# Moving both halves of a query product ahead of the last head's norm, and splitting the last output tile into column halves

## The chip, the cores and the metric

The kernel runs on one core of a Trainium2 chip. The core has five engines with instruction streams of their own: TensorE (PE in the profile; its weight loads are shown as PEld), VectorE (DVE), ScalarE (ACT), GpSimd (POOL) and SyncE (SP), which here only issues DMAs. The engines wait for each other by semaphores. The metric is the device time of one execution in microseconds (us); lower is better.

## The reference, cut to what matters

The kernel computes one layer of an encoder on 1024 tokens and 16 meta tokens, 1024 wide, in float32. Two branches, a neighbourhood attention with 8 heads and a gated recurrence (HGRN2) with 4 heads in both directions, share one input projection. Then come an output projection, an MLP and a last RMSNorm.

```python
def layer(h):                                   # h: (1040, 1024)
    a = rms_norm(h, norm_mix)
    q_na, k_na, v_na, q, z_f, z_b, i, g, gate_na, gate_hg = split(a @ w_in)
    y_na = neighbourhood_attention(q_na, k_na, v_na) @ w_na_out
    o = scan(q, z_f, i) + reverse(scan(reverse(q), ...))
    o = o * rsqrt(mean(o * o) + EPS)            # per head, 128 wide
    y_hg = (o * hg_norm * silu(g)) @ w_hg_out
    h = h + (sigmoid(gate_na) * y_na + sigmoid(gate_hg) * y_hg) @ w_o
    h = h + square(relu(rms_norm(h, norm_mlp) @ w_up)) @ w_down
    return rms_norm(h, norm_final)[16:]
```

## The kernel before, in words

**Products.** A float32 operand is split into a rounded part `hi` and a remainder `lo` (ACT makes `hi`, DVE makes `lo`), and each product is three matmuls, `hi*hi`, `hi*lo` and `lo*hi`, added up in one bank of PSUM (`mm3`, L120 to L124; `mm_pair`, L1395 to L1399). The widest matmul has 512 columns, which fill one bank. `aT[h]` is the normed input, transposed, for token half `h`.

**The join.** The kernel first computes the four recurrent heads (`hgrn`, a generator), then attention for four pairs of heads. At the join three things meet. The last head's tail normalizes its output: squares on ACT (L480), sums on DVE (L482), the root on POOL (L92, L93), the scaled `on` on DVE (L489), for two token halves; then PE transposes each half in four matmuls (`opt`, L493), DVE multiplies by gain and gate into `ot` (L495), and SP stores it (L498). `first_query` (L711) makes attention's first query product, one bank of 24 matmuls for each token half. Behind it come the key product of the first pair, in pieces of 256, 272 and 512 columns, the value product, and the scores (L825, read by DVE at L831).

Here the order on PE, ACT and DVE is the order in which the code is written (`manual_schedule`); on SP and POOL, and later in attention, a scheduler sets it. In every engine's queue an instruction that waits holds back all behind it. The banks of the projection rotate: `mm_cycle` lists two banks called `mm` and, in this stage, one called `mx`; each new product takes the next. A bank can be written again when its readers are done: for a query bank these are ACT's copies (`QX`, L766) and DVE's subtractions (L769). SP's queue holds the two stores of `ot`, then attention's bias (`bs`, L757) and mask (`NB`, L758); POOL subtracts the one from the other (L761), and forms block sums for a later stage (`rt`, L187 to L192).

**The end.** The MLP's second product runs in passes (`ps_` 0 to 3) over pieces of the hidden layer. The last pass adds up four row tiles of 128 rows, columns 512 to 1023, in four banks `bk[0][j]` (two `mm`, two `pa`). Its last two steps are held together (`tail` and `cur`), so that each row tile gets its last twelve matmuls in one go and can be finished while the next is multiplied. `acc[j, 0]` and `acc[j, 1]` hold the residual of the two column halves; `acc[j, 0]` is final long before, and POOL has already multiplied it by the norm's gain `g3` (`half_scaled`). What is left for each row tile is on several engines: DVE adds the bank (L1615), ACT squares and sums (`square`, L1511, a row for the square and one that reads the sum out), POOL adds the other half's sum (L1535) and takes the power -0.5 (L1536), ACT scales the first half (L1538), DVE the second (L1539), and SP stores both (L1540, L1541). On SP, DVE, ACT and POOL the order is again that of the code.

Of the kernel before, what the change touches and what calls it, by code (L numbers as in the profile page):

```python
# [9 lines left out]
F32 = mybir.dt.float32  # L10
F32R = mybir.dt.float32r
I32 = mybir.dt.int32
AF = mybir.ActivationFunctionType
ALU = mybir.AluOpType
# [4 lines left out]
P = 128  # L19
D = 1024  # L20
KC = D // P
T = 1024
TH = 512
# [25 lines left out]
def layer(ctx: ExitStack, tc: tile.TileContext, x, meta, w_in, w_na, w_hg, w_o, w_up, w_dn,  # L49
          g_mix, g_mlp, g_fin, gain, bias, lbl, lmask, wmask, out):  # L50
    nc = tc.nc
    pe, act, dve, pool, sp = nc.tensor, nc.scalar, nc.vector, nc.gpsimd, nc.sync
# [10 lines left out]
    mm_cycle = []  # L63
# [17 lines left out]
    half_c = cp.tile([P, 8], F32, name="half")  # L81
# [629 lines left out]
    def first_query():  # L711

        hi, lo = block_of(C_QN)
        early[C_KN] = block_of(C_KN)
        for h in range(2):
            ps = bank("mm", "mm").rearrange("p a b -> p (a b)")
            for k in range(KC):
                mm3(ps, hi[:, k], lo[:, k], *(t[:, k, :TH] for t in aT[h]), k == 0, k == KC - 1)
            yield ps
    in_order = ExitStack()  # L720
    in_order.enter_context(tc.manual_schedule(engines={e.engine for e in (pe, act, dve)}))
    query = first_query()
    query_ps = [next(query)]
    list(prev)
    query_ps += list(query)
    hps.close()


    gfs = ExitStack()
    gfp = gfs.enter_context(tc.tile_pool(name="gfp", bufs=1, side="right", reuse_waits="tile"))  # L730
    psum_pools(mx=1, s=2, t=2, b=1)
    mm_cycle[1:] = mm_cycle[:0:-1]

    with (tc.tile_pool(name="npr", bufs=1, side="right", reuse_waits="tile") as npr,
          tc.tile_pool(name="np", bufs=1, reuse_waits="tile") as npl):
# [17 lines left out]
        for p in range(NPAIR):  # L753
            NB = npl.tile([P, 2, 1024], F32, tag="NB", name="NB")
            for i in range(2):
# [3 lines left out]
                for o, j0, m in ((0, 0, 3), (432, 1, 2), (720, 0, 2)):  # L759
                    a = NB[:, i, o:o + m * SW].rearrange("p (j c) -> p j c", c=SW)[:, :, :P]  # L760
# [148 lines left out]
    def up_bank(t):  # L909
        return bank(t, t).rearrange("p a b -> p (a b)")  # L910
# [485 lines left out]
    def mm_pair(ps, a, b, q, j, first, last):  # L1396
        for n in range(3):
            pe.matmul(ps, a[n == 2][:, q, j * P:(j + 1) * P], b[n == 1][:, q],  # L1398
                      start=first and n == 0, stop=last and n == 2, skip_group_check=True)  # L1399
# [17 lines left out]
    def half(tag, dt=F32, bufs=1, name=None):  # L1417
        return fp.tile([P, TH], dt, tag=tag, name=name or tag, bufs=bufs)

    def two(tag, dt=F32, bufs=1):  # L1420
        return fp.tile([P, 2, TH], dt, tag=tag, name=tag, bufs=bufs)
# [103 lines left out]
    def half_scaled(i):  # L1525

        y = acc[i, 0]
        pool.tensor_tensor(y, y, g3[:, :TH], op=ALU.mult)
        acc[i, "part"] = fp.tile([P, 1], F32, tag="part", name="part", bufs=4)
        pool.tensor_scalar(acc[i, "part"], acc[i, "ssq"][:, 0:1], 1.0, EPS, op0=ALU.mult, op1=ALU.add)  # L1530

    def finish_half_scaled(i):
        rs = fp.tile([P, 1], F32, tag="rs", name="rs", bufs=4)
        tm = fp.tile([P, 1], F32, tag="rtm", name="rtm", bufs=4)
        pool.tensor_tensor(tm, acc[i, "ssq"][:, 1:2], acc[i, "part"], op=ALU.add)  # L1535
        pool.tensor_tensor(rs, tm, half_c[:, :1], op=ALU.pow)  # L1536
        y = [acc[i, hc] for hc in range(2)]
        act.mul(y[0], y[0], rs)  # L1538
        dve.scalar_tensor_tensor(y[1], y[1], rs, g3[:, TH:], op0=ALU.mult, op1=ALU.mult)  # L1539
        sp.dma_start(out[i * P:(i + 1) * P, :TH], y[0])  # L1540
        sp.dma_start(out[i * P:(i + 1) * P, TH:], y[1])  # L1541

    def after(ps_, bk):
        for j in range(4):
# [37 lines left out]
    with tc.manual_schedule(engines={sp.engine, dve.engine, act.engine, pool.engine}):  # L1582
        us = {n: fetch(*steps[n]) for n in (2, 3)}
        ready = prepare(*steps[2], us.pop(2))
        sp.dma_start(g3, g_fin.rearrange("(o d) -> o d", o=1).broadcast_to([P, D]))
        tail = None
        bk = bk0
        for n, (p_, m) in enumerate(steps):
            if n < 2:
                continue  # L1590
            cur = ready
            if n + 2 < len(steps):
                us[n + 2] = fetch(*steps[n + 2])
            if n + 1 < len(steps):
                ready = prepare(*steps[n + 1], us.pop(n + 1))
            if m == 0:
                bk = down_banks(2 if p_ < 3 else 1)
            if p_ < 3:
                multiply(p_, m, bk, cur)
                if m == NP - 1:  # L1600
                    after(p_, bk)
            elif m < NP // 2 - 2:
                a, b = cur
                for q in range(2):
                    for j in range(4):
                        mm_pair(bk[0][j], a, b, q, j, m == 0 and q == 0, False)
            elif tail is None:
                tail = cur
            else:

                for j in range(4):
                    for e, (a, b) in enumerate((tail, cur)):
                        for q in range(2):
                            mm_pair(bk[0][j], a, b, q, j, False, e == 1 and q == 1)
                    dve.tensor_tensor(acc[j, 1], acc[j, 1], bk[0][j], op=ALU.add)  # L1615
                    square(j, 1)
                    if j:
                        finish_half_scaled(j - 1)
                finish_half_scaled(3)
            side(p_, m)  # L1620


# [53 lines left out]
```

## Time and profile before

| what | value |
|---|---|
| median of three runs | 1527.96 us (1527.82 to 1528.82) |
| the profiled execution | 1527.06 us |
| its span, first to last instruction | 1525.3 us |
| mean granted TensorE clock | 0.999 of full speed |
| PE idle before `opt` (L493), over all four heads | 2.2 us, all ended by DVE's `on` (L489) |
| from 334.0 to 344.2 us: PE, DVE, POOL busy | 8.04, 4.76, 5.51 us |
| from 1518.3 to 1525.3 us: PE, DVE, ACT, POOL busy | 0, 2.10, 2.06, 0.74 us |

A row of the timeline gives the start (us from the span's start), the duration, the engine, the line and operation, what it writes from what it reads, and in brackets how long the engine stood idle before it and what ended that. A row of the groups gives the busy time and the mean duration in ns. The end of a matmul is modelled, and matmuls overlap, so the distance between two starts is the better measure of their cost. In a timeline row several neighbours of one kind can be merged (x4).

### The profile page before, as it was taken

The page shows a single profiled execution, that of the slowest core. Times are in us where ns is not written, and L with a number is a line of the kernel's source. Part 1 is how long each engine was busy: PE and PEld are TensorE (multiplying, and loading weights), DVE is VectorE, ACT ScalarE, POOL GpSimd, SP SyncE. Part 2 cuts the span into 40 slices and gives each one's busy share as a digit, 9 for nine tenths or more (in the row PEclk, how much of TensorE's full clock was granted, in tenths as well). Part 3 has the DMA queues.
Part 4 walks back from the last instruction along what each step waited for, and adds up shares of the span by engine and source line. Part 5 has one row for each costly group of instructions (what it writes and reads, how often), then busy time and mean ns, then how long its engine had stood idle before and what let it go on. Part 6 is the DMA issues. An engine that isn't in the chain of part 4 may idle for free.

```text
span 1525.3 us, 23529 instructions
## 1 busy us (share of the span) xinstructions
PE 1501.0 (98%) x9236; PEld 1254.6 (82%) x9236; DVE 1035.1 (68%) x1608; ACT 657.7 (43%) x1168; POOL 378.5 (25%) x355
## 2 busy tenths in 40 slices
PE   9999999999999999999999999999999999999998
PEld 8888888878888877888888887888888888888886
DVE  7876566655786777666485368877777544877876
ACT  6131313126665576334133235555555533434444
POOL 3313131324404400101000123433333200231142
PEclk9999999999999999999999999999999999999999
DMA  4211011113222227435656123544444676573224
GB/s 168 59 29 57 28 49 37 43 48 112 73 76 94 96 75 237 144 118 187 234 169 217 55 84 131 174 154 152 150 151 157 213 252 234 193 235 111 97 83 152
DMA packets 142591, 195.61 MB, mean 128 GB/s; under 512 B 8192, under 2 KB 90240, under 8 KB 142480
## 3 DMA queue, kind: packets, MB, share of 16 engines
q1 hardware_dynamic: 133216, 172.53, 34.5%
q10 hardware_dynamic: 7088, 14.24, 2.4%
q0 software_dynamic: 2176, 7.34, 1.3%
q8 instruction: 72, 1.18, 0.3%
q14 instruction: 39, 0.32, 0.1%
HBM read 139.56 MB, written 54.53 MB: 127 GB/s over the span
## 4 chain that ended last, share of the span: by engine, by line
PE 86%; DVE 5%; issue 3%; POOL 3%; ACT 2%; DMA 1%; SPq 0%; POOLq 0%; ACTq 0%; DVEq 0%
PE mm L122 10%; PE mm L123 10%; PE mm L124 9%; PE mm L1398 5%; PE pa L1398 4%; PE pb L905 4%; PE pb L906 4%; PE pb L907 4%; PE pb L1398 4%; PE pc L1398 4%; PE pc L905 3%; PE pc L907 3%; PE pc L906 3%; PE pa L905 2%; PE pa L906 2%
## 5 line engine op out<-in xcount | busy, mean ns | idle before, releaser
L122 PE MATMUL mm<-aT,hi 128*128 128x512 f32 (+2 forms) x600 | 214.5, 358 | 0.0
L124 PE MATMUL mm<-aT,lo 128*128 128x512 f32 (+2 forms) x600 | 212.3, 354 | 0.0
L123 PE MATMUL mm<-aT,hi 128*128 128x512 f32 (+2 forms) x600 | 211.3, 352 | 0.0
L97 DVE TENSOR_TENSOR dl<-ur,dh 128x1024 fp32r<-128x1024 f32 x54 | 71.0, 1315 | 87.4 <-ACT dh L96 85.6
L96 ACT CAST dh<-ur 128x1024 fp32r<-128x1024 f32 x54 | 56.9, 1054 | 166.5 <-issue 91.1
L122 PEld LDWEIGHTS mm<-aT,hi 128*128 128x128 f32 x600 | 113.2, 189 | 13.0
L124 PEld LDWEIGHTS mm<-aT,lo 128*128 128x128 f32 x600 | 113.2, 189 | 12.4
L123 PEld LDWEIGHTS mm<-aT,hi 128*128 128x128 f32 x600 | 113.3, 189 | 11.7
L112 ACT CAST hi<-raw 128x1024 fp32r<-128x1024 f32 x34 | 35.7, 1051 | 88.3 <-PE mm L123 78.1
L1203 DVE TENSOR_TENSOR wl<-raw,wh 128x512 fp32r<-128x512 f32 x50 | 40.9, 820 | 36.5 <-ACT wh L1202 36.4
L1207 ACT ACTIVATE uv<-uv 128x512 f32<-128x512 f32 x48 | 30.4, 633 | 80.0 <-DVE uv L1315 48.9
L1203 DVE TENSOR_TENSOR wl<-sx,wh 128x512 fp32r<-128x512 f32 x70 | 61.0, 881 | 3.4 <-ACT wh L1202 3.3
L1202 ACT CAST wh<-sx 128x512 fp32r<-128x512 f32 x70 | 42.2, 620 | 42.2 <-PE pc L906 24.0
L1488 POOL TENSOR_TENSOR w<-w,tt 128x512 f32<-128x512 f32 x16 | 23.4, 1461 | 132.9 <-DVE tt L1487 113.2
L300 POOL TENSOR_TENSOR Y<-X,TN 128x512 f32<-128x512 f32 x20 | 34.3, 1713 | 85.3 <-DVE X L297 85.3
L831 DVE CUSTOM_DVE_ANT_0 pr<-nsc,NB 128x432 f32<-128x432 f32 (+1 forms) x64 | 35.1, 558 | 29.1 <-issue 28.8
L409 DVE TENSOR_TENSOR QQ<-QQ,TN 128x512 f32<-128x512 f32 x48 | 35.1, 740 | 23.7 <-PE sc L404 23.7
L113 DVE TENSOR_TENSOR lo<-raw,hi 128x1024 fp32r<-128x1024 f32 x34 | 47.5, 1398 | 5.2 <-ACT hi L112 5.0
L905 PE MATMUL pb<-nt,wh 128*128 128x512 f32 x128 | 50.2, 392 | 0.3 <-DVE uv L1285 0.2
L122 PE MATMUL mm<-wh,mT 128*128 128x512 f32 x128 | 50.2, 392 | 0.0
L906 PE MATMUL pb<-nt,wh 128*128 128x512 f32 x128 | 49.9, 390 | 0.0
L907 PE MATMUL pb<-nt,wl 128*128 128x512 f32 x128 | 49.8, 389 | 0.0
(408 smaller groups left out, 4443.2 us busy)
## 6 DMA issues: line engine op xcount, KB each, us to landing
raw<-in_w_in SPq DMA_DIRECT2D x56, 512.0 KB, 3.9
ur<-usp SPq DMA_DIRECT2D x54, 512.0 KB, 3.6
raw<-in_w_up SPq DMA_DIRECT2D x16, 1024.0 KB, 6.0
usp<-us SPq DMA_DIRECT2D x60, 256.0 KB, 2.3
sg<-gsp SPq DMA_DIRECT2D x16, 512.0 KB, 4.0
w<-in_w_dn SPq DMA_DIRECT2D x16, 512.0 KB, 4.8
usp<-uv SPq DMA_DIRECT2D x30, 256.0 KB, 2.8
gsp<-gv ACTq DMA_DIRECT2D x24, 256.0 KB, 2.5
```

The lines of the kernel that those rows point to most:

```text
L96: act.copy(hi, src)
L97: dve.tensor_tensor(lo, src, hi.bitcast(F32), op=ALU.subtract)
L113: dve.tensor_tensor(lo[:, :kc], raw[:, :kc], hi[:, :kc].bitcast(F32), op=ALU.subtract)
L122: pe.matmul(ps, lh, rh, start=first, stop=False)
L123: pe.matmul(ps, lh, rl, start=False, stop=False)
L124: pe.matmul(ps, ll, rh, start=False, stop=last)
L905: pe.matmul(ps, lhs[0][:, c], rhs[0][:, k], start=first and k == 0, stop=False, skip_group_check=True)
L906: pe.matmul(ps, lhs[0][:, c], rhs[1][:, k], start=False, stop=False, skip_group_check=True)
L907: pe.matmul(ps, lhs[1][:, c], rhs[0][:, k], start=False, stop=k == 3, skip_group_check=True)
L1202: act.copy(v(hi), src)
L1203: dve.tensor_tensor(v(lo), src, v(hi).bitcast(F32), op=ALU.subtract)
L1398: pe.matmul(ps, a[n == 2][:, q, j * P:(j + 1) * P], b[n == 1][:, q], start=first and n == 0, stop=last and n == 2, skip_group_check=True)
```

## The change

There are two edits. At the join, both halves of `first_query` are now taken before the last head's tail is run (`list(prev)`); before, the second half stood behind it. The rotation of banks is changed with it: before `mm, mx, mm`, now `mx, mm, mm`.

At the end, the last row tile (row 3) is treated apart. Columns 768 to 1023 (`hi`) of its bank are added to `acc[3, 1]` before the last two steps are multiplied, and these steps' products for them go to a new bank of `pc`; columns 512 to 767 stay in the old bank. So the last tile's twelve matmuls of 512 columns become two groups of twelve of 256. The first group's part is added, squared and multiplied by the gain while the second group runs. The first part's sum of squares and that of the first column half go into one extra column of the second part's square: POOL forms their sum times 1024, its root is written as column 257, and ACT's square, which scales by 1/32, then sums all of it. One power follows, and the row is scaled in two pieces: 384 columns on ACT, 640 on DVE (`ylast`, in a tile tagged `tt`), each with one store, the first issued by ACT itself. In all rows the finishing of row j - 1 is now called ahead of the add and the square of row j (`between`).

```diff
-    query = first_query()
-    query_ps = [next(query)]
+    query_ps = list(first_query())
     list(prev)
-    query_ps += list(query)
     hps.close()
...
     psum_pools(mx=1, s=2, t=2, b=1)
-    mm_cycle[1:] = mm_cycle[:0:-1]
+    mm_cycle.insert(0, mm_cycle.pop())
...
-        pool.tensor_tensor(y, y, g3[:, :TH], op=ALU.mult)
+        if i < 3:
+            pool.tensor_tensor(y, y, g3[:, :TH], op=ALU.mult)
+        else:
+            pool.memset(root_c, 0.5)
+            ylast = ends["y"] = two("tt", bufs=2).rearrange("p q t -> p (q t)")[:, :D - SL]
+            pool.tensor_tensor(y[:, :SL], y[:, :SL], g3[:, :SL], op=ALU.mult)
+            pool.tensor_tensor(ylast[:, :P], y[:, SL:], g3[:, SL:TH], op=ALU.mult)
...
-    def finish_half_scaled(i):
+    def finish_half_scaled(i, between=lambda: None):
...
         act.mul(y[0], y[0], rs)
+        between()
         dve.scalar_tensor_tensor(y[1], y[1], rs, g3[:, TH:], op0=ALU.mult, op1=ALU.mult)
...
+    SL, SH = 3 * P, TH // 2
+    root_c = fp.tile([P, 1], F32, name="root_c")
+    lsq = fp.tile([P, 4], F32, name="lsq")
+    ends = {}
+
+    def last_row(products, bk):
+
+        hi, ylast = slice(SH, TH), ends["y"]
+        ysum = half("c5", bufs=4)[:, :SH + 1]
+        y = [acc[3, hc] for hc in range(2)]
+        ps = products(slice(0, SH), bk[0][3])
+        dve.tensor_tensor(y[1][:, :SH], y[1][:, :SH], ps, op=ALU.add)
+        act.activation(half("junk", bufs=2)[:, :SH], y[1][:, :SH], AF.Square, scale=1.0 / 32, accum_out=lsq[:, 0:1])
+        dve.tensor_tensor(ylast[:, P:P + SH], y[1][:, :SH], g3[:, TH:TH + SH], op=ALU.mult)
+        ps2 = products(hi)
+        finish_half_scaled(2, lambda: dve.tensor_tensor(ysum[:, :SH], y[1][:, hi], ps2, op=ALU.add))
+        pool.tensor_scalar(lsq[:, 1:2], lsq[:, 0:1], acc[3, "part"], 1024.0, op0=ALU.add, op1=ALU.mult)
+        pool.tensor_tensor(ysum[:, SH:], lsq[:, 1:2], root_c, op=ALU.pow)
+        act.activation(half("junk", bufs=2)[:, :SH + 1], ysum, AF.Square, scale=1.0 / 32, accum_out=lsq[:, 2:3])
+        dve.tensor_tensor(ylast[:, P + SH:], ysum[:, :SH], g3[:, TH + SH:], op=ALU.mult)
+        pool.tensor_tensor(lsq[:, 3:4], lsq[:, 2:3], half_c[:, :1], op=ALU.pow)
+        act.mul(y[0][:, :SL], y[0][:, :SL], lsq[:, 3:4])
+        dve.tensor_scalar(ylast, ylast, lsq[:, 3:4], None, op0=ALU.mult)
+        act.dma_start(out[3 * P:4 * P, :SL], y[0][:, :SL])
+        sp.dma_start(out[3 * P:4 * P, SL:], ylast)
...
-                for j in range(4):
+                def products(j, cols, ps=None):
+                    new = ps is None
+                    if new:
+                        ps = up_bank("pc")
+                    dst = ps[:, :SH] if new else ps[:, cols]
                     for e, (a, b) in enumerate((tail, cur)):
                         for q in range(2):
-                            mm_pair(bk[0][j], a, b, q, j, False, e == 1 and q == 1)
-                    dve.tensor_tensor(acc[j, 1], acc[j, 1], bk[0][j], op=ALU.add)
+                            mm_pair(dst, a, [t[:, :, cols] for t in b], q, j, new and e == q == 0, e == 1 and q == 1)
+                    return dst
+
+                y1 = acc[3, 1][:, SH:]
+                dve.tensor_tensor(y1, y1, bk[0][3][:, SH:], op=ALU.add)
+                for j in range(3):
+                    products(j, slice(0, TH), bk[0][j])
+                    def add():
+                        dve.tensor_tensor(acc[j, 1], acc[j, 1], bk[0][j], op=ALU.add)
+
+                    if j:
+                        finish_half_scaled(j - 1, add)
+                    else:
+                        add()
                     square(j, 1)
-                    if j:
-                        finish_half_scaled(j - 1)
-                finish_half_scaled(3)
+                last_row(lambda *a: products(3, *a), bk)
```

PE at the join, before: the last three matmuls of the first query half (`aT_87` and `aT_88` belong to token half 0), the eight transposes of the last head's output, and the first of the second half.

```order
L122 MATMUL mm<-aT_87,hi 128x512
L123 MATMUL mm<-aT_88,hi 128x512
L124 MATMUL mm<-aT_87,lo 128x512
L493 MATMUL opt<-ident,on 128x128 x8
L122 MATMUL mm<-aT_89,hi 128x512
L123 MATMUL mm<-aT_90,hi 128x512
L124 MATMUL mm<-aT_89,lo 128x512
```

The same transposes in the changed kernel: ahead of them stand the last matmuls of the second query half, behind them the first key piece.

```order
L122 MATMUL mm<-aT_89,hi 128x512
L123 MATMUL mm<-aT_90,hi 128x512
L124 MATMUL mm<-aT_89,lo 128x512
L493 MATMUL opt<-ident,on 128x128 x8
L122 MATMUL mm<-aT_87,hi 128x256
L123 MATMUL mm<-aT_88,hi 128x256
L124 MATMUL mm<-aT_87,lo 128x256
```

So the transposes moved behind 24 matmuls; the rest of PE's order, up to the last row tile, is as it was, and so is that of the other engines here.

ACT at the end of the program, before: squares (L1511) and scalings (L1538) of the four row tiles.

```order
L1511 ACTIVATE junk,fsq<-hr 128x512 x2
L1538 ACTIVATE hr<-hr,rs 128x512
L1511 ACTIVATE junk,fsq<-hr 128x512
L1538 ACTIVATE hr<-hr,rs 128x512
L1511 ACTIVATE junk,fsq<-hr 128x512
L1538 ACTIVATE hr<-hr,rs 128x512 x2
```

ACT at the same place in the changed kernel, whose lines for them are L1510 and L1543; L1561 and L1567 are the two squares of the last row tile.

```order
L1510 ACTIVATE junk,fsq<-hr 128x512
L1543 ACTIVATE hr<-hr,rs 128x512
L1510 ACTIVATE junk,fsq<-hr 128x512
L1543 ACTIVATE hr<-hr,rs 128x512
L1510 ACTIVATE junk,fsq<-hr 128x512
L1561 ACTIVATE junk,lsq<-hr 128x256
L1543 ACTIVATE hr<-hr,rs 128x512
L1567 ACTIVATE junk,lsq<-c_14290 128x257
L1570 ACTIVATE hr<-hr,lsq 128x384
L1572 DMA out<-hr 128x384
```

Each scaling of row j - 1 stands now ahead of the square of row j, and row 2's stands between the two squares of row 3.

DVE behind its last split of operands, in the changed kernel: the early half-row add (L1654), the adds of rows 0 to 2 (L1658), their scalings (L1545), and row 3's own operations.

```order
L1654 TENSOR_TENSOR hr<-hr,pa 128x256
L1658 TENSOR_TENSOR hr<-hr,mm 128x512 x2
L1545 SCALAR_TENSOR_TENSOR hr<-hr,rs,g_12043 128x512
L1658 TENSOR_TENSOR hr<-hr,pa 128x512
L1545 SCALAR_TENSOR_TENSOR hr<-hr,rs,g_12043 128x512
L1560 TENSOR_TENSOR hr<-hr,pa 128x256
L1562 TENSOR_TENSOR tt<-hr,g_12043 128x256
L1564 TENSOR_TENSOR c_14290<-hr,pc 128x256
L1545 SCALAR_TENSOR_TENSOR hr<-hr,rs,g_12043 128x512
L1568 TENSOR_TENSOR tt<-c_14290,g_12043 128x256
L1571 TENSOR_SCALAR tt<-tt,lsq 128x640
```

Before, the list was two adds, a scaling, an add, a scaling, an add and two scalings, all of 512 columns. POOL's list behind row 2's root has a tensor_scalar, the extra column's root and the last root, where a sum and a root stood.

## The prediction

> **What bounds the kernel now.** I read the page first, then the timeline of single engines at the two edited places.
>
> ```profile
> PE 1501.0 (98%) x9236; PEld 1254.6 (82%) x9236; DVE 1035.1 (68%) x1608; ACT 657.7 (43%) x1168; POOL 378.5 (25%) x355
> PE 86%; DVE 5%; issue 3%; POOL 3%; ACT 2%; DMA 1%; SPq 0%; POOLq 0%; ACTq 0%; DVEq 0%
> ```
>
> TensorE (PE) is busy 98% of the span, and 86% of the chain that ended last is its own work. Time can be won only where TensorE stands still, or after its last matmul. Both edits aim at such places. The first is the join between the recurrent part and attention:
>
> ```profile
> 335.04 0.40 PE L124 MATMUL mm<-aT,lo 128*128 128x512 f32 x1
> 336.75 0.66 PE L493 MATMUL opt<-ident,on 128*128 128x128 f32 x4 [1.31 <-DVE on L489]
> 338.25 0.65 PE L493 MATMUL opt<-ident,on 128*128 128x128 f32 x4 [0.84 <-DVE on L489]
> 338.66 0.48 PE L122 MATMUL mm<-aT,hi 128*128 128x512 f32 x1
> 338.97 0.40 PE L123 MATMUL mm<-aT,hi 128*128 128x512 f32 x1
> ...
> 343.97 0.39 PE L124 MATMUL mm<-aT,lo 128*128 128x512 f32 x1
> 344.20 0.28 PE L122 MATMUL mm<-aT,hi 128*128 128x256 f32 x1
> ...
> 347.07 0.29 PE L122 MATMUL mm<-aT,hi 128*128 128x272 f32 x1
> ```
>
> The first query half ends, two groups of four transposes (L493) wait for VectorE (DVE), then the second half runs from 338.66, and the key product begins at 344.20. The second place is the end:
>
> ```profile
> 1515.39 0.39 PE L1398 MATMUL pa<-dh 128*128 128x512 f32 x1
> ...
> 1517.88 0.39 PE L1398 MATMUL pa<-dh,dl 128*128 128x512 f32 x1
> 1519.09 0.63 ACT L1511 ACTIVATE junk<-hr 128x512 f32<-128x512 f32 x1 [1.38 <-DVE hr L1615]
> 1519.62 0.19 ACT L1511 ACTIVATION_READ_ACCUMULATOR junk<-hr 128x1 f32 x1
> 1520.16 0.55 POOL L1536 TENSOR_TENSOR rs<-rtm,half 128x1 f32<-128x1 f32 x1
> 1520.74 0.75 DVE L1539 SCALAR_TENSOR_TENSOR hr<-hr,rs,g 128x512 f32<-128x512 f32 x1 [1.08 <-POOL rs L1536]
> 1520.45 0.33 SPq L1540 DMA_DIRECT2D out<-hr  x1
> ...
> 1521.49 0.33 SPq L1540 DMA_DIRECT2D out<-hr  x1
> 1521.91 0.41 SPq L1541 DMA_DIRECT2D out<-hr  x1
> GB/s 0 0 72 358 440 379 410 379 440 144 41 0 0 0 0 0 215 379 430 379 430 389 420 379 440 379 430 389 430 154 0 0 0 0 0 0 0 0 0 0
> ```
>
> The matmuls end at 1518.27, and the span ends at 1525.3: 7 us of add, square, root, scale and store. The last line is the DMA rate from 1518 to 1526 in slices of 0.2 us: the stores of rows 2 and 3 run as one block from about 1521.2 to 1523.95, near 400 GB/s, and 1.35 us follow it.
>
> **Part 1, the join.** From 335.04 to 344.20 pass 9.16 us. If nothing waits, these hold: one slot of the first half, 0.23; 24 matmuls of 512 columns at (344.20 - 338.97) / 23 = 0.227, so 5.46; two groups of four transposes at 338.66 - 338.25 = 0.41, so 0.82; and one slot after transposes that is longer by 0.31 - 0.23 = 0.08. Sum 6.59, so **2.57 us** go if the eight transposes find their input ready. They do: in the new order they come at 335.27 + 24 x 0.227 = 340.7, and their input is ready at 338.2:
>
> ```profile
> 337.50 0.69 DVE L489 TENSOR_TENSOR on<-po,hrs 128x512 f32<-128x512 f32 x1 [0.81 <-POOL hrs L93]
> 338.11 1.58 DVE L495 SCALAR_TENSOR_TENSOR ot<-opt,gain_sb,gs 128x512 f32<-128x512 f32 x2
> 339.72 1.39 DVE L769 TENSOR_TENSOR QX<-mm,QX 64x512 fp32r<-64x512 f32 x2
> ```
>
> What is late next is DVE. The `ot` operations now start with the transposes, near 341.4 in place of 338.1, and the query subtractions (L769) are queued behind them: two `ot` to 342.8, the first half's subtractions to 344.2. This bank is now wanted by the second key piece, the one of 272 columns, and the new rotation gives the first key piece the free bank `mx`. The first piece starts at 344.20 - 2.57 = 341.63 and takes 347.07 - 344.20 = 2.87, so the second wants its bank at 344.5: 0.3 us to spare. If that cover is gone, the cost is what DVE is later.
>
> The SyncE (SP) queue is in order too. It stores the two `ot` before it loads attention's bias and mask, so those slip with `ot`, from its end at 339.7 to 342.8, by 3.1 us; GpSimd (POOL), which subtracts the bias and then forms block sums, slips with them:
>
> ```profile
> 352.52 2.42 POOL L761 TENSOR_TENSOR NB<-NB,bs 128x384 f32<-128x384 f32 x3
> 368.01 1.28 POOL L187 TENSOR_TENSOR rt<-aT,aT 128x512 f32<-128x512 f32 x1 [3.68 <-DMA tsp_t<-rt]
> 367.46 0.46 DVE L831 CUSTOM_DVE_ANT_0 pr<-nsc,NB 128x288 f32<-128x288 f32 x1 [7.28 <-issue]
> 368.37 2.00 DVE L113 TENSOR_TENSOR lo<-raw,hi 128x1024 fp32r<-128x1024 f32 x1
> 322.11 1.22 DVE L113 TENSOR_TENSOR lo<-raw,hi 128x1024 fp32r<-128x1024 f32 x1
> ```
>
> The mask is finished at 354.94 + 3.1 = 358.0, and its first reader (L831) comes at 367.46 - 2.6 = 364.9: covered by 6.9 us. But the block sums now end some 5.7 us later against the scores, and a GpSimd operation beside a DVE one costs: L113 took 2.00 us beside L187, 1.22 alone. One such overlap (0.78) is there already; one or two more may come, in DVE time of which TensorE's fillers cover most. I take **+0.1**, between 0 and 0.78. Everything later hangs on TensorE's order, which is the same, so the rest of the gain is carried to the end.
>
> **Part 2, the last row.** The twelve last matmuls, 0.227 apart, become 24 of 256 columns, which at the key piece's 2.87 / 24 = 0.12 take 2.88 in place of 2.72: the end moves by **+0.16** to 1518.43. The early add of the half row into `y1` stands on DVE ahead of row 0's add, where DVE idled:
>
> ```profile
> 1511.51 0.69 DVE L1615 TENSOR_TENSOR hr<-hr,mm 128x512 f32<-128x512 f32 x1 [0.98 <-PE mm L1398]
> 1513.36 0.55 POOL L1536 TENSOR_TENSOR rs<-rtm,half 128x1 f32<-128x1 f32 x1
> 1513.65 0.63 ACT L1511 ACTIVATE junk<-hr 128x512 f32<-128x512 f32 x1 [0.64 <-DVE hr L1615]
> 1514.28 0.71 ACT L1538 ACTIVATE hr<-hr,rs 128x512 f32<-128x512 f32 x1
> L858 DVE TENSOR_TENSOR PT<-ppt,PT 128x256 fp32r<-128x256 f32 x8 | 3.3, 410 | 0.0
> L1518 POOL TENSOR_SCALAR rtm<-fsq 128x1 f32<-128x1 f32 x4 | 4.5, 1122 | 6.8 <-ACT junk L1511 6.6
> L1519 POOL TENSOR_TENSOR rs<-rtm,half 128x1 f32<-128x1 f32 x4 | 3.6, 896 | 0.3
> L1536 POOL TENSOR_TENSOR rs<-rtm,half 128x1 f32<-128x1 f32 x4 | 2.2, 548 | 0.3
> L1535 POOL TENSOR_TENSOR rtm<-fsq,part 128x1 f32<-128x1 f32 x4 | 0.9, 215 | 15.9 <-ACT junk L1511 15.9
> L784 ACT CAST KS<-KS 64x256 fp32r<-64x256 f32 x16 | 6.5, 405 | 0.2
> L784 ACT CAST KS<-KS 64x512 fp32r<-64x512 f32 x8 | 4.9, 617 | 0.1
> L559 DVE TENSOR_SCALAR xt<-xt,rs 128x1024 f32<-128x1024 f32 x8 | 6.0, 754 | 2.3 <-POOL rs L563 2.1
> ```
>
> It costs about 0.41 (L858, half width); DVE is free from 1511.51 - 0.98 = 1510.5, so it is over by 1511 and hidden.
>
> The hidden price is the order on ScalarE (ACT): the scaling of row j - 1 now stands ahead of the square of row j. Row 0's root ends at 1513.91, its scaling starts at 1513.95, and as an ACT row overlaps the one before by 0.1 (1519.09 + 0.63 against 1519.62), row 1's square, which ran at 1513.65, starts at 1514.56. From a square's start to its read-out's end are 0.72 us, from there to the root's start 0.35 (1519.81 to 1520.16), and the root takes 0.55. So: square 1 read out at 1515.3, root 1 at 1516.2, scaling 1 holds ACT to 1516.8, square 2 is read out at 1517.5, root 2 is ready at 1518.45.
>
> The last half's add is ready at 1518.47 + 0.41 = 1518.9, but its square waits for two more things. ACT is held by row 2's scaling from 1518.5 to 1519.1. And on GpSimd the extra column comes after root 2: 0.07 to take over (0.35 less L1535's 0.22, halved), a tensor_scalar that I price at 0.22 (L1535, with no product of DVE beside it yet), 0.07, and a root at 0.90 (L1519, whose four ran beside 128x512 products like the one that row 2 now has at 1518.8). That gives 1519.7. The square of 257 columns is read out 0.72 - 0.21 = 0.51 later (L784, half width against full), at 1520.2; the last root needs 0.07 + 0.55: 1520.85. DVE's product of 640 columns lies between half of the 1024-column L559 (0.38) and all of it (0.75); I take 0.6, the nearer by width: 1521.5, and SP issues the store at about 1521.55. ACT scales its 384 columns beside it and issues its own store. Before, the last issue came at 1521.91: **0.35 us earlier**.
>
> Row 2's stores leave at about 1519.2 and 1519.6 and stand no longer ahead of row 3's 512 KB. These need 1.3 us at 400 GB/s from 0.7 after the issue (1520.45 to 1521.2 before), so they end near 1523.6 in place of 1523.95. I take **-0.3**. Ends: -0.65 with 0.55 for the column's root; +0.6 with 1.12 (L1518) for its tensor_scalar.
>
> The widest term here is GpSimd's. The rows give 0.90 for a root beside DVE's product with both operands in SBUF, 0.55 without. The Trainium skill, page "SBUF — State Buffer", section "Who interferes with whom", has a rule that speaks against this change: VectorE with two SBUF inputs and GpSimd reading SBUF exclude each other, and whoever is first keeps the port for its whole instruction. By that rule the root would wait for the end of row 2's product (1518.8 + 0.75) and then take its 0.55: 1520.1 in place of 1519.7, and the sum would be -2.4, 1525.6, which is where the second rival's range begins. The trace agrees in direction only, with 0.90 against 0.55.
>
> **Sum.** -2.57 + 0.1 - 0.3 = **-2.8 us**. On the profiled execution, 1527.06 with 1525.3 of span and 1.8 around it, that is 1524.3. The runs' median, 1527.96, lies 0.9 above that execution, so **1525.2** on their scale. About 0.2%, or 3.06 us, is what a measurement can tell from no change, so 1524.9 and 1531.0 are the bounds.
>
> **Rivals.**
> 1. *The column's root is not disturbed.* The root costs 0.55, and the tail gives -0.65. Against it: row 2's product is due at 1518.8, just before the root. Total -2.57 + 0.1 - 0.65 = -3.1, 1524.8 (1524.2 to 1524.9). Chance 0.27.
> 2. *GpSimd is held back at the extra column.* Tensor_scalar 1.12, root 0.90: the tail is +0.6, the total -1.9, 1526.1 (1525.6 to 1526.4). For it: all four L1518 with a per-row scalar were long. Against: those all had DVE beside them from the start. Chance 0.15.
> 3. *The join does not do what it says.* The second key piece waits for DVE's subtractions. The spare is 0.3 us; if `ot` and the subtractions come a whole subtraction pair (1.39) later, 1.1 of the 2.57 goes back, 1526.3; the far end is 1527.5. Chance 0.08.
> 4. *Slower: the displaced GpSimd block collides with the softmax.* Three GpSimd operations of 1.3 us fall behind the first score in place of one; if each holds DVE in full and TensorE with it, 3 x 1.3 = 3.9 is paid against 2.87 won: +1.0, 1529.0. It decides once more than 2.9 us of TensorE idle is new between 365 and 376. Against it: the one now there leaves under 0.8 on DVE. Chance 0.05.
>
> My forecast (1524.8 to 1525.6) keeps 0.45; a fifth of it lies below 1524.9. Faster by over 0.2%: 0.27 + 0.08 = 0.35. Slower by over 0.2% needs more collisions than rival 4's three; I leave 0.03 of its 0.05 to that. Within: 0.62. The range 1524.2 to 1526.8 leaves out the far ends of rivals 3 and 4 and what lies below rival 1.
>
> **What would show it.** Step 1: the L493 transposes, near 340.7, with no idle before them, and the first key matmul 2.5 us earlier; wrong if the second key piece shows idle. The first score on DVE near 364.9. Step 2: last matmul 0.16 later against row 2's; row 1's square 0.9 later; the extra column's root longer than 0.55; last store issue 0.3 earlier against the last matmul's old place. The forecast fails if TensorE idles anew in the softmax, or if the span after the last matmul is not 6.5 us (6.1 to 7.4).

## The result, and the profile after

| | before | changed |
|---|---|---|
| median of the runs made side by side | 1527.50 us (13 runs) | 1524.79 us (13 runs) |
| the same once more | 1527.94 us (25 runs) | 1524.83 us (11 runs) |
| profiled execution; its span | 1527.06; 1525.3 us | 1524.48; 1522.7 us |
| first query matmul behind the scan's last `po` group to first key matmul | 9.70 us | 7.04 us |
| second key piece to the same transpose behind the first softmax | 53.50 us | 54.21 us |
| row 2's last matmul to the end of the span | 10.14 us | 10.27 us |

The table counts from these rows of before, the first query matmul and row 2's last matmul; row 2's last matmul in the changed kernel stands with its end below.

```profile
334.50 0.47 PE L122 MATMUL mm<-aT,hi 128*128 128x512 f32 x1
1515.16 0.39 PE L1398 MATMUL pa<-dh,dl 128*128 128x512 f32 x1
```

The ratio of the runs is 0.9984, with a 95% interval of 0.9976 to 0.9992: 2.4 us off 1528, between 1.2 and 3.7. The second set gives 0.9985 (0.9976 to 0.9994). The forecast was 2.8 us. The medians differ by 2.7 and 3.1. The kernel is faster, by the join; the edit of the last row tile as a whole gave nothing, and at the first softmax, between the two, something was lost. In the changed kernel line numbers are one lower than before in the middle of the program (L768 was L769, L834 was L835), and the end has numbers of its own.

The page of the changed kernel first, busy time and instructions of each engine:

```profile
PE 1501.2 (99%) x9248; PEld 1255.7 (82%) x9248; DVE 1037.4 (68%) x1612; ACT 658.3 (43%) x1170; POOL 380.8 (25%) x358
```

TensorE's busy time is what it was (1501.0), in a span that is 2.6 shorter: what went is standing still. The timeline of PE at the join in the changed kernel, then that of DVE:

```profile
333.73 0.39 PE L474 MATMUL po<-SB,QQ 128*128 128x128 f32 x2
333.88 0.47 PE L122 MATMUL mm<-aT,hi 128*128 128x512 f32 x1
...
340.13 1.03 PE L493 MATMUL opt<-ident,on 128*128 128x128 f32 x8
340.92 0.36 PE L122 MATMUL mm<-aT,hi 128*128 128x256 f32 x1
343.87 0.29 PE L122 MATMUL mm<-aT,hi 128*128 128x272 f32 x1
```

```profile
340.76 1.41 DVE L495 SCALAR_TENSOR_TENSOR ot<-opt,gain_sb,gs 128x512 f32<-128x512 f32 x2 [3.19 <-PE opt L493]
342.20 2.82 DVE L768 TENSOR_TENSOR QX<-mm,QX 64x512 fp32r<-64x512 f32 x4
```

All eight transposes stand in one row, with no idle time ahead of them. The second key piece starts 3.20 earlier than before (347.07). Of this 0.63 was there already ahead of the join (the last `po` group, L474, started at 334.36 before): it has nothing to do with the change. The join itself gave 2.58. (The first key matmul came 2.66 nearer to the first query matmul, 7.04 for 9.70; the first slot behind the transposes is 0.08 longer.) DVE's first two subtractions (half of 2.82) end at 343.6, and the second key piece wants their bank at 343.87: nothing waits.

At the first softmax the changed kernel's timeline shows what the displaced GpSimd block does:

```profile
364.58 1.29 POOL L191 TENSOR_TENSOR rt<-rt 128x512 f32<-128x512 f32 x1
369.67 1.28 POOL L187 TENSOR_TENSOR rt<-aT,aT 128x512 f32<-128x512 f32 x1 [2.95 <-DMA tsp_t<-rt]
```

```profile
364.26 0.46 DVE L830 CUSTOM_DVE_ANT_0 pr<-nsc,NB 128x288 f32<-128x288 f32 x1 [6.76 <-issue]
365.18 1.77 DVE L113 TENSOR_TENSOR lo<-raw,hi 128x1024 fp32r<-128x1024 f32 x1
369.78 1.34 DVE L834 TENSOR_SCALAR pr<-pr,rc 128x288 f32<-128x288 f32 x1
```

```profile
371.26 0.41 PE L845 MATMUL ppt<-ident,pr 128*128 128x128 f32 x2 [0.66 <-DVE rc L833]
398.08 0.41 PE L845 MATMUL ppt<-ident,pr 128*128 128x128 f32 x2 [0.35 <-DVE pr L834]
```

Before, one DVE operation ran beside this block: L113, 2.00 in place of 1.22. Now it is two: L113 takes 1.77, beside L191, and the scaling L834, 0.36 when nothing is beside it, takes 1.34, because GpSimd's L187 began 0.11 ahead of it. In all seven profiles of kernels with the join's edit in which SP loads attention's bias and mask, as here, the scaling ends 0.16 to 0.18 behind that L187, so its length (0.68 to 1.34) goes by when L187 began. TensorE waits for that scaling (0.66, new), and a wait of 0.45 for the scores is gone. The lead over before, 3.20 at the first score, is 2.49 at the transposes near 398.

The end of the changed kernel, row 2's last matmul on PE and behind it ACT, POOL and DVE and the queues that store:

```profile
1512.43 0.39 PE L1397 MATMUL pa<-dh,dl 128*128 128x512 f32 x1
1514.12 0.62 ACT L1510 ACTIVATE junk<-hr 128x512 f32<-128x512 f32 x1
1514.75 0.42 DVE L1562 TENSOR_TENSOR tt<-hr,g 128x256 f32<-128x256 f32 x1
1514.91 0.32 POOL L1540 TENSOR_TENSOR rtm<-fsq,part 128x1 f32<-128x1 f32 x1 [1.45 <-ACT junk L1510]
1515.30 0.55 POOL L1541 TENSOR_TENSOR rs<-rtm,half 128x1 f32<-128x1 f32 x1
1515.95 0.27 POOL L1565 TENSOR_SCALAR lsq<-lsq,part 128x1 f32<-128x1 f32 x1
1516.07 0.75 DVE L1545 SCALAR_TENSOR_TENSOR hr<-hr,rs,g 128x512 f32<-128x512 f32 x1
1516.30 0.92 POOL L1566 TENSOR_TENSOR c<-lsq,root_c 128x1 f32<-128x1 f32 x1
1517.26 0.42 ACT L1567 ACTIVATE junk<-c 128x257 f32<-128x257 f32 x1 [0.65 <-POOL c L1566]
1517.84 0.56 POOL L1569 TENSOR_TENSOR lsq<-lsq,half 128x1 f32<-128x1 f32 x1 [0.62 <-ACT junk L1567]
1518.43 0.55 DVE L1571 TENSOR_SCALAR tt<-tt,lsq 128x640 f32<-128x640 f32 x1 [1.28 <-POOL lsq L1569]
1519.01 0.33 SPq L1573 DMA_DIRECT2D out<-tt  x1
1519.08 0.35 ACTq L1572 DMA_DIRECT2D out<-hr  x1
```

The chain runs from square 2 (1514.12) over row 2's sum and root and the extra column's root (0.92) to the square that waits for it, the last root, the product and the two stores. The last issue is 6.65 behind row 2's last matmul; before, it was 6.75. The DMA rate from 1515 to 1523 in slices of 0.2 us shows the rest:

```profile
GB/s 225 358 420 359 359 430 369 103 0 0 41 0 205 369 410 369 400 379 389 92 10 0 0 0 307 384 374 376 420 315 369 77 0 0 0 0 0 0 0 0
```

The last row's 512 KB start at 1519.8, 0.8 after the first issue, and flow until 1521.3; the span ends 1.4 later.

### The profile page after: what moved, and what is told of

It is laid out like the page before. It is cut to its first block, busy times and chain, and to the rows that moved or that the text cites. A ratio compares the mean times of both kernels' runs of the same rounds, so it can differ in the third digit from the quotient of the medians.

```text
span 1522.7 us, 23561 instructions
## 1 busy us (share of the span) xinstructions
PE 1501.2 (99%) x9248; PEld 1255.7 (82%) x9248; DVE 1037.4 (68%) x1612; ACT 658.3 (43%) x1170; POOL 380.8 (25%) x358
## 5 line engine op out<-in xcount | busy, mean ns | idle before, releaser
L113 DVE TENSOR_TENSOR lo<-raw,hi 128x1024 fp32r<-128x1024 f32 x34 | 46.8, 1378 | 5.2 <-ACT hi L112 5.0
L122 PE MATMUL mm<-wh,mT 128*128 128x512 f32 x128 | 50.2, 392 | 0.0
L124 PE MATMUL mm<-wh,mT 128*128 128x512 f32 x128 | 49.8, 389 | 0.0
```

The costliest lines, as they stand in the source:

```text
L113: dve.tensor_tensor(lo[:, :kc], raw[:, :kc], hi[:, :kc].bitcast(F32), op=ALU.subtract)
L122: pe.matmul(ps, lh, rh, start=first, stop=False)
L124: pe.matmul(ps, ll, rh, start=False, stop=last)
```

## The experiments

**The parts apart.** The first kernel is the one before with the join's hunks alone:

```diff
-    query = first_query()
-    query_ps = [next(query)]
+    query_ps = list(first_query())
     list(prev)
-    query_ps += list(query)
...
-    mm_cycle[1:] = mm_cycle[:0:-1]
+    mm_cycle.insert(0, mm_cycle.pop())
```

> The join's edit alone (order and rotation), the end as before. Theory: the join carries the whole gain. From the last L122 of the first query half to the first key matmul 7.0 us as in the changed kernel (9.7 before), the second key piece without idle, new idle of 0.66 on TensorE at the first softmax's reciprocal (L833 of the changed kernel), and from row 2's last matmul to the span's end 10.1 as before. Total 1.9 to 2.6 us under before, the changed kernel's time within 0.3. By the prediction's sum, in which the end gives 0.3, this kernel would be 0.3 slower than the changed one.

Measured: ratio 0.9985 (0.9975 to 0.9994), median 1525.34 beside 1528.32. From the first query matmul to the key product 7.03 us, from row 2's last matmul to the end 10.08, and TensorE's new wait at the first softmax is there (0.54). By the ratio the size of the gain is that of the whole change; the last few tenths between this kernel and the changed one cannot be told apart by the runs.

The second kernel is the changed one with these hunks undone, so that only the end is new.

> The end's edit alone, the join as before. Theory from the changed kernel's trace: 9.7 us from the first query half to the first key matmul with both waits of L493 there, no new idle at the first softmax, and from row 2's last matmul to the span's end 10.2 to 10.3, so 0.1 slower than before in the span (0 within what the runs can tell). The prediction's step says 9.8, so 0.3 faster than before.

Measured: ratio 0.9997 (0.9988 to 1.0007). The runs cannot separate +0.1 from -0.3, but the profile can: row 2's last matmul at 1516.64, the end of the span at 1526.9, 10.26 apart as in the changed kernel, where the prediction had 9.84. No new wait stands at the first softmax. One thing was not as expected: the join took 11.3 us in this profile, not 9.7, with the same two waits. This is taken up at the end.

**The rotation.** The changed kernel with the old order of banks:

```diff
-    mm_cycle.insert(0, mm_cycle.pop())
+    mm_cycle[1:] = mm_cycle[:0:-1]
```

> The changed kernel with the old rotation of banks (mm, mx, mm), so that the first key piece gets the first query half's bank. Theory: the rotation is needed; the first key piece waits for DVE's subtractions from that bank, which end near 343.6 in the changed trace, where its first matmul starts at 340.9: 2.5 to 2.9 us of idle ahead of the first key matmul, ended by DVE on L768, and the join's gain is gone (total within 0.4 of before). Rival: the rotation is of no consequence, no idle there, and the time is the changed kernel's.

PE's timeline in this kernel has the wait where the theory put it:

```profile
340.15 1.04 PE L493 MATMUL opt<-ident,on 128*128 128x128 f32 x8
343.77 0.35 PE L122 MATMUL mm<-aT,hi 128*128 128x256 f32 x1 [2.58 <-DVE QX L768]
```

From the first query matmul to the first key matmul it takes 9.88 us, beside 9.70 before, and its span is 1525.1 in its one execution, beside 1525.3. So the moved code alone gives nothing: the wait moves from `on` to the query bank. The second line of the edit is what makes the first one pay.

**The collision in the softmax.** In the changed kernel the first pair's bias and mask stand on SP's queue behind the stores of `ot`. Here ACT issues them:

```diff
-                sp.dma_start(bs, bias[:, (2 * p + i) * 384:(2 * p + i + 1) * 384])
-                sp.dma_start(NB[:, i, :1008], wmask)
+                load = (sp if p else act).dma_start
+                load(bs, bias[:, (2 * p + i) * 384:(2 * p + i + 1) * 384])
+                load(NB[:, i, :1008], wmask)
```

> The changed kernel with the first pair's bias and mask loaded from ACT's queue in place of SP's, where they stand behind the two stores of ot. Theory: the late start of GpSimd's block costs 0.6 to 0.7 in the first softmax. Then the subtractions of the mask (L760) begin at least 2.5 us earlier than in the changed kernel (347.6), the block sums L187 no longer run beside the first row's scaling (L834), which goes back from 1.34 to about 0.5, and the idle of 0.66 ahead of it goes: from the first key matmul to a matmul behind the first softmax 0.5 to 0.7 less. Rival: the idle there is set by DVE's own order (its L113 of 1.2 us ahead of it) and stays; then the distance is the same within 0.2, or another collision takes its place.

The timeline of this kernel, POOL and DVE:

```profile
361.27 1.28 POOL L187 TENSOR_TENSOR rt<-aT,aT 128x512 f32<-128x512 f32 x1 [2.63 <-DMA tsp_t<-rt]
```

```profile
365.21 1.22 DVE L113 TENSOR_TENSOR lo<-raw,hi 128x1024 fp32r<-128x1024 f32 x1
369.76 0.36 DVE L835 TENSOR_SCALAR pr<-pr,rc 128x288 f32<-128x288 f32 x1
```

GpSimd's last block sum is over before the first score, and both DVE operations are back to their undisturbed times (1.22, 0.36). TensorE's wait is gone, and from the second key piece to the transposes near 398 it takes 53.09 us in place of 54.21, below the 53.50 of before too, where one overlap stood. But row 2's last matmul came no earlier (1512.52, beside 1512.43), so this kernel was then timed, beside the changed kernel itself.

> The changed kernel once more, unaltered, on the same chip as the two runs beside it, so that they can be compared by their medians. It should repeat its first result, 2.0 to 3.0 under before, with 0.5 to 0.7 of new idle on TensorE at the first softmax.

> The run with bias and mask from ACT's queue, now timed. Theory: the collision at the first softmax costs the whole kernel what it costs there, so the median is 0.6 to 1.1 under that of the changed kernel. Rival, as its first profile had it: that gain is taken back by the wait for a weight load at 709 (idle of 1.06 there), and the median is within 0.3 of the changed kernel's.

Measured: 1524.83 for the changed kernel, 1524.93 for the one with the bias on ACT. The rival holds: what is won at the softmax does not reach the end. The timeline of PE in this kernel's second profile, then in the one before and the changed one, shows one place where it goes:

```profile
398.84 0.41 PE L846 MATMUL ppt<-ident,pr 128*128 128x128 f32 x2 [0.36 <-DVE pr L835]
711.12 0.50 PE L905 MATMUL pb<-at,hi 128*128 128x512 f32 x1 [1.52 <-DVE gv L998]
921.48 0.51 PE L905 MATMUL pc<-nT,wh 128*128 128x512 f32 x1 [0.62 <-ACT wh L1202]
```

```profile
400.57 0.41 PE L846 MATMUL ppt<-ident,pr 128*128 128x128 f32 x2 [0.35 <-DVE pr L835]
712.00 0.50 PE L905 MATMUL pb<-at,hi 128*128 128x512 f32 x1 [0.53 <-DVE gv L998]
922.30 0.50 PE L905 MATMUL pc<-nT,wh 128*128 128x512 f32 x1 [0.58 <-ACT wh L1202]
```

```profile
709.42 0.50 PE L904 MATMUL pb<-at,hi 128*128 128x512 f32 x1 [0.63 <-DVE gv L997]
919.72 0.50 PE L904 MATMUL pc<-nT,wh 128*128 128x512 f32 x1 [0.62 <-ACT wh L1201]
```

Near 710 TensorE waits for DVE, behind ACT's casts of loads that SP issues there. With the edit this wait was 1.06 and 1.52; without it, 0.63 and 0.32 in the changed kernel's two profiles. The instructions near 710 are the same. From the second key piece (345.76 in this profile) to the matmul near 920 there are 575.7 us, and 575.8 and 576.0 in the changed kernel's two profiles: of the 0.7 to 1.1 that the softmax gave 0.1 to 0.2 is left. Near 570 the clock is halved for some 3 us in part of the profiles (see the last section), so pairs that are alike there are the better test: this profile and the changed kernel's first, both without it, and the two others, both with it. In the one pair the lead is 1.13 behind the softmax, 1.06 at a wait near 594, 0.19 near 710 and 0.13 near 920; in the other 0.72, 0.89, 0.14 and 0.13. So it is lost between 594 and 710.

**The end.** Two edits aim at the two suspects there. One puts each row's add and square ahead of the finishing of the row before, as it was before the change:

```diff
-                    if j:
-                        finish_half_scaled(j - 1, add)
-                    else:
-                        add()
+                    add()
                     square(j, 1)
+                    if j:
+                        finish_half_scaled(j - 1)
```

> The changed kernel with each row's add and square ahead of the finishing of the row before, as before the change (row 3's own order is kept). Theory: the new order on ACT, scaling j - 1 ahead of square j, is what makes the extra column late. Against row 2's last matmul: row 2's square at +1.2 in place of +1.7, its root ready 0.5 earlier, the extra column's root begins at +3.3 in place of +3.9, ahead of row 2's product on DVE, and takes 0.55 to 0.7 in place of 0.92; the last store is issued 0.6 to 1.0 earlier (+5.6 to +6.0 in place of +6.6), and the span ends 0.6 to 1.0 earlier against that matmul (10.27 in the changed kernel). Rival: the order on ACT is hidden behind the last half's add; then the last store comes within 0.2 of the changed kernel's.

The other takes one operand of DVE's products out of SBUF:

```diff
-        dve.scalar_tensor_tensor(y[1], y[1], rs, g3[:, TH:], op0=ALU.mult, op1=ALU.mult)
+        dve.scalar_tensor_tensor(y[1], y[1], rs, ends["g"], op0=ALU.mult, op1=ALU.mult)
...
-        dve.tensor_tensor(ylast[:, P:P + SH], y[1][:, :SH], g3[:, TH:TH + SH], op=ALU.mult)
+        dve.tensor_tensor(ylast[:, P:P + SH], y[1][:, :SH], ends["g"][:, :SH], op=ALU.mult)
...
-        dve.tensor_tensor(ylast[:, P + SH:], ysum[:, :SH], g3[:, TH + SH:], op=ALU.mult)
+        dve.tensor_tensor(ylast[:, P + SH:], ysum[:, :SH], ends["g"][:, SH:], op=ALU.mult)
...
                 tail = cur
+                ends["g"] = up_bank("pb")
+                act.copy(ends["g"], g3[:, TH:])
```

> The changed kernel with the second half of the gain copied once to a bank of PSUM, which DVE's products of the row tiles (L1545, L1562, L1568) read in place of SBUF; nothing else is moved. Theory: GpSimd's small operations are long beside DVE only where both of DVE's operands come from SBUF. Then the extra column's root takes 0.55 in place of 0.92 and row 2's sum of squares 0.19 in place of 0.32, at the same places, and the last store is issued 0.3 to 0.5 earlier. Rival: any DVE work beside them does it; then 0.9 and 0.3 stay, and so does the end.

The extra column's root in the first of these kernels, with the product that comes after its start, and the last store:

```profile
1515.78 0.55 POOL L1566 TENSOR_TENSOR c<-lsq,root_c 128x1 f32<-128x1 f32 x1
1516.02 0.74 DVE L1545 SCALAR_TENSOR_TENSOR hr<-hr,rs,g 128x512 f32<-128x512 f32 x1
1518.33 0.34 ACTq L1572 DMA_DIRECT2D out<-hr  x1
```

And in the second, where `pb` is the bank that holds the gain:

```profile
1514.75 0.19 POOL L1540 TENSOR_TENSOR rtm<-fsq,part 128x1 f32<-128x1 f32 x1 [1.45 <-ACT junk L1510]
1515.92 0.74 DVE L1545 SCALAR_TENSOR_TENSOR hr<-hr,rs,pb 128x512 f32<-128x512 f32 x1
1516.02 0.55 POOL L1566 TENSOR_TENSOR c<-lsq,root_c 128x1 f32<-128x1 f32 x1
1518.42 0.34 ACTq L1572 DMA_DIRECT2D out<-hr  x1
```

Both theories hold. In the second kernel the root runs beside the same product, begun 0.10 into it (0.23 in the changed kernel), and takes 0.55: here it is the second operand in SBUF that costs, not DVE's work as such. In us behind row 2's last matmul:

| kernel | square 2 | root 2 ready | column's root, its length | last issue | end of span |
|---|---|---|---|---|---|
| before | 1.21 | 2.83 | none | 6.75 | 10.14 |
| changed | 1.69 | 3.42 | 3.87, 0.92 | 6.65 | 10.27 |
| squares first | 1.21 | 2.83 | 3.40, 0.55 | 5.95 | 9.62 |
| gain in PSUM | 1.69 | 3.29 | 3.74, 0.55 | 6.14 | 9.72 |
| both, and bias on ACT | 1.21 | 2.83 | 3.40, 0.55 | 5.80 | 9.56 |

The row of the squares first has the split tile with ACT's old order for rows 0 to 2. Beside before, its end is 0.52 nearer (9.62 for 10.14). So the split paid, and the new order of ACT that came with it took 0.65 away again.

**Together.** All three edits on the changed kernel, and the two of the end alone; the last pair ran on one chip.

> All three edits (bias and mask from ACT's queue, squares ahead of the finishing, gain in PSUM) on the changed kernel. Theory: the two places add up, the first softmax gives 0.6 to 1.0 and the end 0.7 to 1.2 against row 2's last matmul, so 1.3 to 2.2 under the changed kernel and 3.5 to 5 under before: faster than both. Rival: what the softmax gives is taken back by a wait for a load before 710, where the run with the bias alone stood no earlier than the changed kernel; then only the end's 0.7 to 1.2 is left, about 3 to 3.6 under before.

> The changed kernel with the two edits of the end (squares ahead of the finishing, gain in PSUM), bias and mask as in the changed kernel. Theory: from row 2's last matmul to the span's end 9.5 to 9.6 as in the run with all three, 0.7 under the changed kernel's 10.27, and the median 0.5 to 0.9 under the changed kernel's. Rival: the profiled gain of the end is not carried into the median, which stays within 0.3.

> The kernel with all three edits once more, beside the one without the bias edit on the same chip. Theory (the softmax's gain is taken back at the loads near 700 to 710): the medians of the two lie within 0.4 of each other, and the profile of this kernel has no idle of over 0.25 on TensorE at the first softmax. Rival (the gain lasts): this one is 0.6 to 1.1 lower.

> The kernel with the two edits of the end alone, for the same pair: 0.9 to 1.1 under the changed kernel's 1524.8 again, with 0.5 to 0.7 of idle at the first softmax, and within 0.4 of the run with all three by the theory, 0.6 to 1.1 above it by the rival.

| kernel | median, us | beside before | ratio (95%) |
|---|---|---|---|
| all three | 1523.77 | 1528.36 | 0.9974 (0.9965 to 0.9983) |
| the end's two | 1523.80 | 1527.94 | 0.9976 (0.9966 to 0.9985) |
| all three, again | 1523.80 | 1527.65 | 0.9978 (0.9969 to 0.9987) |
| the end's two, again | 1524.34 | 1527.65 | 0.9980 (0.9971 to 0.9989) |

All three edits came 1.0 under the changed kernel's 1524.8, timed on another chip, and not 1.3 to 2.2; that is nearer to the rival. The end's two edits give 1.0 under the changed kernel on the same chip (1523.80 and 1524.83), near the 0.7 of the profile; the intervals of the two ratios overlap. In their second run they came 0.5 under 1524.8, where 0.9 to 1.1 was expected. All four medians lie under those of every other kernel that was timed in rounds, 3.3 to 4.6 under before's. What the bias adds stays open: nothing in one pair (1524.93 and 1524.83), 0.54 in the other (1523.80 and 1524.34), which lies between what the theory and the rival had. In the four profiles with the bias on ACT the wait near 710 is 1.06, 1.52, 0.30 and 0.95; in the other changed kernels it is at most 0.63. Why the loads there land late in three of four was not found.

## Why the prediction was right, step by step

The time was right: 1525.2 was forecast, with 1524.2 to 1526.8, and 1524.8 came out. The steps were not all right. That the difference came out so near, 2.7 by the medians for 2.8, is in part luck: the term for the end is 0.43 too good, and a loss of clock in the runs of before (last section) that no term held works the other way. By its own sign, TensorE idling anew in the softmax, the prediction was to fail; that idling came (0.66), and the time held all the same, because little of it was carried to the end.

**The join, -2.57.** Measured -2.58, and alone it gives the whole gain. The transposes were due at 340.7 and stood, with the 0.63 that lies ahead, at 340.13. The spare for the second key piece was put at 0.3 and is 0.26. That the rotation is part of the step was right, and the rotation's run shows its price, 2.58. The third rival is out.

**The softmax, +0.1 between 0 and 0.78.** The mechanism was right, the size at the spot was not. The step said that TensorE's fillers would cover most of DVE's lost time. They cover part of it for a large split like L113: before, it was 0.78 longer, and TensorE waited 0.45 behind it (53.50 us with this overlap, 53.09 in the kernel with none). The second overlap fell on the scaling L834, which TensorE waits for next. From the second key piece to the transposes near 398 the seven profiles named above (the join's edit, bias and mask on SP) took 53.5 to 54.2 us, 53.9 in the mean, with L834 between 0.68 and 1.34; before took 53.5, the end alone 53.3. So 0 to 0.7 was lost at the spot, 0.4 in the mean, within the bound and above the value taken. By the matmul near 920 little of that is left: 575.2 us from the second key piece before, 574.8 to 576.0 in the seven, 575.5 in the mean. Three of the seven have the halved clock near 570 (575.7 in the mean); the four that have none, like before, come to 575.3. So what was carried on was between 0 and +0.2, near the value taken, though not for the reason given. The sentence that everything later hangs on TensorE's order, so that a gain is carried to the end, was too simple: it held for the join's gain, and not for the bias edit's. The fourth rival is out.

**The end, -0.3.** Measured +0.13; this is the term that was mis-sized. TensorE's part was right (+0.15 for +0.16), as was the price of ACT's order (square 1 later by 0.93 for 0.91). Then small things add up. Row 2's sum took 0.32 beside DVE's product L1562 in place of 0.19, so root 2 came 0.13 later than forecast (3.42 for 3.29). The column's tensor_scalar took 0.27 for 0.22; its root took 0.92 for 0.90; the steps between are some hundredths longer each, and the last root was ready 5.97 behind row 2's last matmul in place of 5.69. With the product at 0.55 for 0.6 SP's issue came at 6.58 for 6.39. (That 0.6 was a guess: between 0.38 for 512 columns and 0.75 for 1024, 640 columns come to 0.47 by width.) From there to the end of the span the step had 3.45 and the trace has 3.69: 0.8 to the first data, 1.5 for 512 KB, 1.4 behind them, each a little more than the numbers of before that it was built on. Sum: 0.19 + 0.24 = 0.43, which is the whole error. The largest price in this term, ACT's order, was seen and rightly sized for row 1; what it cost the end, 0.65, was never set against the split's own gain. The first rival (a root of 0.55) and the second (a tensor_scalar of 1.12) are both out.

By the Trainium skill's page "SBUF — State Buffer", section "Who interferes with whom", the root would have waited for the end of the product: 1516.82 and 0.55 more, so 1517.37. It was over at 1517.22, 0.15 sooner, and the measurement decides. The same section says that VectorE with at most one input in SBUF, outside its two-port modes, does not contend, and that a tensor_scalar can enter such a mode, with the later one blocked to the end of the earlier. The run with the gain in PSUM (0.55) agrees with the first. L834 agrees with the second in kind: it waited for GpSimd's L187 and ended 0.17 behind it, which again is sooner, by 0.19, than its own 0.36 would have it.

In the profile the parts add up as -0.63 ahead of the join, -2.58, +0.71, -0.24 between 398 and row 2's last matmul, and +0.13: the 2.6 of the spans. Without the first, and with the 0 to 0.2 that is carried in place of the two in the middle, the change is worth 2.25 to 2.45 by the profiles, and the two ratios say 2.4 and 2.3. By this count the forecast of 2.8 was 0.35 to 0.55 too good, nearly all of it by its last term. The runs can't confirm that: the interval, 1.2 to 3.7, holds all these values, and the medians say 2.7 and 3.1.

## What to carry to other kernels

Moving independent work ahead of a wait pays only if the buffer that the next work needs comes free as early: check the rotation along with the order. Time won or lost in the middle of a program can be taken back at a later wait for a load, so it has to be read at the end or from medians, not at the spot: here the join's 2.58 was carried past those waits, the softmax's 0.7 to 1.1 was not. On a tail of small operations, look at what runs beside each, and price a new order apart from the split that it comes with: here the split was worth 0.52, and the order of ACT's squares alone (0.65) undid it.

## What was not expected of the hardware

The run with the end alone has this at the join, in PE's timeline, and in the windows of PE (length, busy time with matmuls, granted clock, DMA share, GB/s):

```profile
336.53 0.66 PE L493 MATMUL opt<-ident,on 128*128 128x128 f32 x4 [1.31 <-DVE on L489]
338.03 0.84 PE L493 MATMUL opt<-ident,on 128*128 128x128 f32 x4 [0.85 <-DVE on L489]
...
341.23 0.63 PE L122 MATMUL mm<-aT,hi 128*128 128x512 f32 x1
341.66 0.46 PE L123 MATMUL mm<-aT,hi 128*128 128x512 f32 x1
341.95 0.39 PE L124 MATMUL mm<-aT,lo 128*128 128x512 f32 x1
342.18 0.39 PE L122 MATMUL mm<-aT,hi 128*128 128x512 f32 x1
```

```profile
334.00:345.00 11.00, 8.85 (x38) 0.84 0.43 134
```

After the two waits the matmuls come 0.43 apart in place of 0.23 for some 3.3 us, the granted clock of this stretch is 0.84, and the second transposes are 7.57 from the first key matmul in place of 5.95: 1.6 us lost to a halved clock after 2.2 us of idle time. The profile of before has the same waits and no such stretch, and the rotation's run has a wait of 2.58 and none, so it does not come every time; a like stretch follows the idle time of 2.35 near 570 in 7 of these 14 profiles. The runs fit that. Of 79 runs of before in these experiments 31 have a mean granted clock of 0.996 or 0.997, and their means are 1529.2 and 1528.3 us, against 1526.6 at 0.999; so have 3 of 10 of the run with the end alone, and 6 of 86 timed runs of the kernels whose join does not wait. But the mean does not say where the clock was lost: the second profile with the bias on ACT has 0.997, and lost it in the first 20 us, behind a wait of 1.36. Removing the wait at the join thus seems to have removed a chance of this loss too, which no term of the prediction held. It is not the whole gain: at the same mean clock of 0.998, 34 runs of before have a mean of 1527.7 us and 19 of the changed kernel 1525.1. That it is the idle time that brings the loss on fits all of this, but was not tried by itself.

The Trainium skill, page "TensorE: Matmul & The Clock Gate", section "HAM oscillation — how this bites in real kernels", gives the rule as no idle gaps of TensorE above about 3.4 us. Here the clock was halved behind gaps of 1.31 and 0.85, and behind one of 2.35, all below that figure; whether the gaps did it is open.
